# A diffusion backbone step on one core: a weight split that asks for its own load only, and four steps a unit for the last part of the S5 build

## The chip, the cores and the metric

The kernel runs on one core of a Trainium2 chip, in one launch. The metric is the time of one execution on the device in microseconds (us), the median of several runs. In this text PE is the matrix engine (TensorE), PEld its weight loads, DVE the vector engine, ACT the scalar engine, POOL GpSimd, and SP the engine that does nothing here but issue DMAs. Every engine works through its own instructions in the order in which they stand; so does SP: a DMA that must wait for its buffer holds up every DMA behind it.

## The reference, cut to what matters

One step of a two-layer network over 640 tokens (128 context tokens and 512 latent ones) of width 1024. Everything is float32.

```
for layer in (0, 1):
    mod = silu(cond) @ ada_w[layer] + ada_b[layer]        # 6 vectors of 1024 for each of two conditions
    h = rmsnorm(x) * (1 + scale) + shift
    if layer == 0:
        y = [pooling mixer | gated short convolution](h @ ab_w_in) @ ab_w_out
    else:
        q, k, v, u = split(h @ cd_w_in)
        y = [attention(q, k, v) | gelu, glu of S5(u)] @ cd_w_out
    x = x + gate * y
    x = x + gate2 * (relu(h2 @ mlp_w1) ** 2 @ mlp_w2)
```

S5 is a linear recurrence in both directions with complex coefficients: `state[t] = lam_bar * state[t-1] + b_bar @ u[t]`, `y[t] = Re(c @ state[t]) + d * u[t]`. Its matrices are parameters of the layer and depend on no token.

## The kernel before, in words

**Layout.** The activations stand transposed in SBUF, eight chunks of 128 features by 640 tokens, the tokens in two halves of 320. The weights come in 178 units of 128x1024 (512 KB each), used in a fixed order. Each float32 product is made of three fast ones: the unit's high part `wh` and low part `wl`, and the same of the activation, in the order (wl, high), (wh, high), (wh, low). A whole unit is 48 matmuls of 320 columns, a half of one 24.

**The stream of weights.** `load` (L249) issues on SP the DMAs of the next units into tiles `raw` (two buffers; units 2 and 3 have buffers of another tag), as far as `ahead` units beyond the next to be split. `split` (L258) takes the next unit: ACT copies `raw` into `wh` (L266), and `wl = raw - wh` follows on DVE (L271) for the units listed in `ON_VECTOR`, on POOL (L273) for the others. There are four `wh`/`wl` pairs, so a unit is split when the unit four places before it is retired. `turn(u)` (L293) is what the main loops call after unit u: it calls `load()` first, then splits without loading further. Other callers are `retire` from `in_units` (L505) and from `glu`, and the start-up (`start`, L541), which splits units 0 to 3 by hand.

**The order of the work.** Each engine's instructions stand in the order in which the Python code emits them. Layer 0: units 0 to 15 (input projection), 16 to 23 (output projection), 24 to 87 (the MLP in four blocks of 16 units). The last block's second half is units 80 to 87: `out_units` (L459) takes 80 to 83 whole, then 84 to 87 once for the first half of the tokens and once more for the second. After every residual add the square of the new x is summed for the norm: ACT squares (L391), POOL adds (`acc`, L392). Layer 1: units 88 to 91 give the S5 input u (`in_units`), 92 and 93 the first q and k, 94 to 97 the v projection, the rest the other q and k with attention between them.

**The S5 build.** The matrices of the recurrence are built from the parameters while the MLP of layer 0 runs. `s5_build` (L936) is a generator; each `yield` ends a small step. Between two MLP units the loop's `step` pumps it 2 or 3 steps (4 while the coefficients are not built). Its last part, from the `store()` after the loop over b (L1044) on, rearranges 1 MB through DRAM: eight DMAs `ast<-kst` (L1047), then for f = 0 to 7 a load `at<-ast` (L1053), a copy on POOL that permutes it (`a2`, L1058; the profile names it a), and a DMA `ast2<-a2` back to DRAM (L1016). The tiles `at` and `a2` have two buffers each. What is not done when the MLP ends is emitted in one piece by `n.pump(1000)`, before `layer1`.

**The entry of layer 1.** `layer1` (L1065) issues on SP, behind what is left of the build: the cached keys and values, four tiles `et` of the build's result, the load of unit 93, and two stores `xst` that put half of x away. `in_units` then runs units 88 to 91; its evacuation writes u to DRAM in another order (`uds<-uf`, issued by ACT, L1216) and reads it back (`up<-uds`, SP, L1220), a chunk of 128 rows at a time. Unit 92's eight k steps have the first S5 products between them: `s5_in(b)` (L1236) multiplies `et` by `up` on PE (L1242) into one of two PSUM banks, ACT (L1247) and DVE (L1249) empty the bank, and SP loads `et` of b + 4. `s5_in` 0 to 3 stand at k = 5, 6, 7 and 7 of unit 92, 4 to 15 in pairs at k = 1 to 6 of unit 93.

Of the kernel before, what the change touches and what calls it, by code (L numbers as in the profile page):

```python
# [205 lines left out]
class Net:  # L206
# [51 lines left out]
    def split(self, ahead=True):  # L258
        u = self.n_split
        if u == self.n_units or len(self.wt) == 4:  # L260
            return
        self.load()
        raw = self.raw.pop(u)
        wh = self.ws.tile([128, 1024], F32R, name="wh")
        wl = self.ws.tile([128, 1024], F32R, name="wl")
        self.nc.scalar.activation(wh, raw, AF.Copy)  # L266
        self.wt[u] = (wh, wl)
        self.n_split += 1
        if u in ON_VECTOR:
            self.pend.add(u)  # L270
            self.defer(lambda: self.nc.vector.tensor_sub(wl, raw, wh.bitcast(F32)))  # L271
        else:
            self.nc.gpsimd.tensor_sub(wl, raw, wh.bitcast(F32))  # L273
        if ahead:
            self.load()
# [671 lines left out]
    def s5_build(self):  # L947
# [66 lines left out]
        def store():  # L1014
            for o, i in stores:
                nc.sync.dma_start(o, i)  # L1016
            stores.clear()

        F = None
        for b in range(17):  # L1020
# [12 lines left out]
            if b < 16:  # L1033
# [8 lines left out]
                cplx(F, self.pa, self.bc[:, 2:4], 2 * b, 1)  # L1042
                yield
        store()  # L1044
        yield
        for t in range(8):
            nc.sync.dma_start(ast[:, t], self.kst[:, :, 16 * t:16 * t + 128].rearrange("n g c -> g n c"))  # L1047
# [500 lines left out]
def _emit(tc, A):  # L1548
    from contextlib import ExitStack
    with ExitStack() as ctx:  # L1550
        n = Net(tc, A, ctx)
        pts = n.start()
        n.bg = n.s5_build()

        n.step = lambda: n.ada_step(1 if n.n_ada < 40 else 0)
        n.built, n.np = False, 1
        n.layer0(pts)

        def step():
            if n.n_ada < 48:  # L1560
                n.ada_step(2)
            else:
                n.spare = None
                n.ada_step(0 if not n.built else 1)
                n.pump(4 if not n.built else 3 if n.np % 8 == 0 else 2)
                n.np += n.built

        n.step = step
        n.mlp(0, 24, n.norm(0, 3, C_N2), n.norm(1, 0, C_N1))
        n.ada_step(96)  # L1570
        n.pump(1000)
        n.step = lambda: None
        n.layer1(88, n.norm(1, 0, C_N1), n.norm(1, 3, C_N2))
        n.step = lambda: n.late(2)
        n.mlp(1, 114, n.norm(1, 3, C_N2), n.final)
        n.stats_half(1)
        n.spread()
        n.final(1, range(KC))
# [15 lines left out]
```

## Time and profile before

| what | value |
|---|---|
| time, median of 3 runs | 1484.7 us |
| lowest, highest | 1480.81, 1505.91 us |
| the profiled execution's own time | 1483.03 us |
| its span in the trace | 1481.3 us |
| PE busy | 1428.6 us (96% of the span) |
| DVE, POOL, ACT busy | 882.5, 587.8, 484.7 us |
| HBM traffic | 170.5 MB read, 22.5 MB written |

The span is the time from the first to the last instruction of the profiled execution; 1.7 us of its own time lie around it. A busy PE is not PE at full pace: its clock, the granted clock of the profile, has two levels, 1.0 (2.4 GHz) and 0.5 (1.2 GHz), and a stretch's value is a mean of the two. Waits of PE show as idle time, half pace only as a lower clock.

### The profile page before, as it was taken

What the parts mean: (1) busy time and instruction counts of PE and PEld (TensorE: products, weight loads), DVE (VectorE), ACT (ScalarE), POOL (GpSimd) and SP (SyncE); (2) the same over time, 40 slices, a digit from 0 to 9 for tenths busy, and PEclk for the clock granted to TensorE, in tenths of its full rate; (3) what the DMA queues carried; (4) which work ended last, traced back from release to release, by engine and by line L of the source; (5) the groups of instructions that cost most, each with busy time, mean ns of one, the idle gap of its engine ahead of it and who ended that gap; (6) DMA issues with size and microseconds to landing.
All of it is one profiled execution on the core that took longest, in us unless ns stands there. A gap on an engine that the chain in (4) does not pass through costs nothing.

```text
span 1481.3 us, 24120 instructions
## 1 busy us (share of the span) xinstructions
PE 1428.6 (96%) x9757; PEld 1397.0 (94%) x9757; DVE 882.5 (60%) x1618; ACT 484.7 (33%) x856; POOL 587.8 (40%) x429
## 2 busy tenths in 40 slices
PE   7999999999999999999989999999999999999997
PEld 7999899999999999999988888998999999999996
DVE  7899986889988888844539764427541211211213
ACT  4321234312423432433433445535322312311321
POOL 2333021326788679734324321050433333333341
PEclk9999999999999999999999999999999999999998
DMA  9245531514544545524673323521532222222211
GB/s 377 86 174 175 185 129 59 186 57 142 194 173 152 176 169 175 178 83 155 224 219 127 99 80 101 201 72 58 169 116 72 72 86 72 72 81 76 73 58 71
DMA packets 73966, 193.30 MB, mean 131 GB/s; under 512 B 15360, under 2 KB 23936, under 8 KB 73344
## 3 DMA queue, kind: packets, MB, share of 16 engines
q1 hardware_dynamic: 68976, 188.99, 37.8%
q10 hardware_dynamic: 4880, 2.78, 0.6%
q8 instruction: 77, 1.26, 0.4%
q14 instruction: 33, 0.27, 0.1%
HBM read 170.51 MB, written 22.54 MB: 130 GB/s over the span
## 4 chain that ended last, share of the span: by engine, by line
PE 73%; DVE 13%; issue 5%; ACT 3%; POOL 2%; DMA 2%; SPq 0%; ACTq 0%; DVEq 0%; POOLq 0%
PE pp L304 64%; DVE condb L335 3%; PE bk L1437 2%; DVE wl L271 1%; PE pp L1319 1%; DVE x L449 1%; PE pp L1504 1%; PE bk L1242 1%; DVE hl L443 1%; PE pp L1419 1%; ACT wh L266 1%; PE pp L1391 1%; DMA raw<-wts 1%; PE bk L999 1%; DVE pb L681 1%
## 5 line engine op out<-in xcount | busy, mean ns | idle before, releaser
L273 POOL TENSOR_TENSOR wl<-raw,wh 128x1024 fp32r<-128x1024 f32 x112 | 277.3, 2480 | 605.2 <-ACT wh L266 545.0
L304 PE MATMUL pp<-hh,wl 128*128 128x320 f32 x1472 | 360.6, 316 | 9.7 <-ACT hh L437 6.3
L304 PE MATMUL pp<-hl,wh 128*128 128x320 f32 x1472 | 355.4, 312 | 2.2 <-DVE hl L636 2.0
L304 PE MATMUL pp<-hh,wh 128*128 128x320 f32 x1472 | 354.3, 311 | 0.0
L266 ACT ACTIVATE wh<-raw 128x1024 fp32r<-128x1024 f32 x178 | 186.3, 1051 | 327.3 <-PE pp L304 234.0
L304 PE MATMUL pp<-dh,wl 128*128 128x320 f32 x1152 | 280.1, 310 | 5.6 <-DVE x L449 2.7
L304 PE MATMUL pp<-dh,wh 128*128 128x320 f32 x1152 | 278.0, 309 | 0.0
L304 PE MATMUL pp<-dl,wh 128*128 128x320 f32 x1152 | 278.0, 309 | 0.0
L304 PEld LDWEIGHTS pp<-hh,wl 128*128 128x128 f32 x1472 | 251.9, 190 | 14.1 <-ACT hh L437 7.0
L304 PEld LDWEIGHTS pp<-hl,wh 128*128 128x128 f32 x1472 | 252.9, 190 | 3.7 <-DVE hl L636 2.8
L304 PEld LDWEIGHTS pp<-hh,wh 128*128 128x128 f32 x1472 | 253.0, 190 | 0.0
L449 DVE SCALAR_TENSOR_TENSOR x<-pp,mod,x 128x128 f32<-128x128 f32 (+2 forms) x240 | 91.5, 433 | 241.6 <-PE pp L304 241.3
L304 PEld LDWEIGHTS pp<-dh,wl 128*128 128x128 f32 x1152 | 195.9, 188 | 8.8 <-issue 5.6
L304 PEld LDWEIGHTS pp<-dl,wh 128*128 128x128 f32 x1152 | 196.6, 188 | 0.3 <-DVE dl L454 0.3
L304 PEld LDWEIGHTS pp<-dh,wh 128*128 128x128 f32 x1152 | 196.5, 188 | 0.0
L335 DVE SCALAR_TENSOR_TENSOR condb<-ada,condb 128x1024 bf16<-128x1024 f32 x124 | 182.7, 1474 | 2.4
L775 DVE SCALAR_TENSOR_TENSOR pp<-pp,t 128x640 f32<-128x640 f32 x64 | 53.1, 830 | 179.9 <-ACT t L774 179.9
L774 ACT ACTIVATE t<-pp 128x640 f32<-128x640 f32 x64 | 45.1, 704 | 253.4 <-PE pp L304 238.5
L392 POOL TENSOR_TENSOR acc<-acc,sq 128x320 f32<-128x320 f32 (+1 forms) x36 | 40.0, 1112 | 129.6 <-ACT sq L391 121.4
L271 DVE TENSOR_TENSOR wl<-raw,wh 128x1024 fp32r<-128x1024 f32 x66 | 90.0, 1363 | 0.0
L391 ACT ACTIVATE sq<-x 128x320 f32<-128x320 f32 (+1 forms) x51 | 29.1, 570 | 113.4 <-DVE x L449 107.0
L777 DVE TENSOR_TENSOR dl<-pp,dh 128x640 fp32r<-128x640 f32 x64 | 52.6, 822 | 3.9 <-DVE pp L775 0.5
(249 smaller groups left out, 1601.2 us busy)
## 6 DMA issues: line engine op xcount, KB each, us to landing
raw<-wts SPq DMA_DIRECT2D x178, 512.0 KB, 3.5
ada<-ada SPq DMA_DIRECT2D x80, 512.0 KB, 4.4
spare<-ada SPq DMA_DIRECT2D x16, 512.0 KB, 3.5
est<-s5e SPq DMA_DIRECT2D x16, 256.0 KB, 4.6
fst<-s5fc SPq DMA_DIRECT2D x16, 256.0 KB, 4.5
et<-est SPq DMA_DIRECT2D x16, 256.0 KB, 3.7
ft<-fst SPq DMA_DIRECT2D x8, 512.0 KB, 4.1
x<-x SPq DMA_DIRECT2D x8, 320.0 KB, 5.2
```

The costliest lines, as they stand in the source:

```text
L266: self.nc.scalar.activation(wh, raw, AF.Copy)
L271: self.defer(lambda: self.nc.vector.tensor_sub(wl, raw, wh.bitcast(F32)))
L273: self.nc.gpsimd.tensor_sub(wl, raw, wh.bitcast(F32))
L304: self.nc.tensor.matmul(o, a[:, w], b[:, s], start=first and n == 0, stop=last and n == 2)
L335: self.nc.vector.scalar_tensor_tensor(self.junk, a, 1.0, self.condb[:, c], op0=OP.mult, op1=OP.mult, accum_out=self.mod[:, l, j, f, c:c + 1])
L391: self.nc.scalar.activation(q, self.x[f][:, s], AF.Square)
L392: (self.nc.vector if f >= last else self.nc.gpsimd).tensor_add(self.acc[:, s], self.acc[:, s], q)
L449: self.nc.vector.scalar_tensor_tensor(self.x[f][:, s], p[:, s.start - 320 * h:s.stop - 320 * h], self.mod[:, l, j, f, c:c + 1], self.x[f][ ...
L774: self.nc.scalar.activation(t, p, AF.Relu)
L775: self.nc.vector.scalar_tensor_tensor(p, p, 0.0, t, op0=OP.max, op1=OP.mult)
L777: self.defer(lambda: self.nc.vector.tensor_sub(dl, p, dh.bitcast(F32)))
L1437: nc.tensor.matmul(po[:, 64 * h:64 * (h + 1)], pT[:, h, 128 * b:128 * (b + 1)], vv[:, hs], start=b == 0, stop=b == len(vs) - 1)
```

## The change

`split` calls `load(1)` where it called `load()`, which is `load(2)`: before it splits unit u it makes sure that unit u is loaded, and no longer issues the load of u + 1. After `turn` it makes no difference, since `turn` has called `load()` itself. And from the end of the build's loop over b on, a new flag `turning` makes `step` pump four build steps where it pumped two or three.

```
     def split(self, ahead=True):
         u = self.n_split
         if u == self.n_units or len(self.wt) == 4:
             return
-        self.load()
+        self.load(1)
...
         store()
+        self.turning = True
         yield
         for t in range(8):
             nc.sync.dma_start(ast[:, t], self.kst[:, :, 16 * t:16 * t + 128].rearrange("n g c -> g n c"))
...
-        n.built, n.np = False, 1
+        n.built, n.turning, n.np = False, False, 1
...
-                n.pump(4 if not n.built else 3 if n.np % 8 == 0 else 2)
+                n.pump(4 if n.turning or not n.built else 3 if n.np % 8 == 0 else 2)
```

PE, DVE and ACT have the same instructions in the same order before and after; only POOL and SP differ, POOL in one place. On POOL, during units 81 to 83 and the half passes of 84 to 87, there stood before (wl of units 85, 86 and 87, the copies L1058, and the sums `acc`):

```order
L273 TENSOR_TENSOR wl_6740<-raw_6706,wh_6739 128x1024
L392 TENSOR_TENSOR acc_6704<-acc_6704,sq_6805 128x640
L273 TENSOR_TENSOR wl_6811<-raw_6737,wh_6810 128x1024
L1058 COPY a2_6816<-at_6751 128x4x8x16
L392 TENSOR_TENSOR acc_6704<-acc_6704,sq_6870 128x640
L273 TENSOR_TENSOR wl_6876<-raw_6808,wh_6875 128x1024
L1058 COPY a2_6882<-at_6814 128x4x8x16
L392 TENSOR_TENSOR acc_6704<-acc_6704,sq_6911 128x320
L392 TENSOR_TENSOR acc_6704<-acc_6704,sq_6941 128x320
```

The same place on POOL now (the copies' line is L1059):

```order
L273 TENSOR_TENSOR wl_6740<-raw_6706,wh_6739 128x1024
L1059 COPY a2_6755<-at_6751 128x4x8x16
L392 TENSOR_TENSOR acc_6704<-acc_6704,sq_6809 128x640
L273 TENSOR_TENSOR wl_6815<-raw_6737,wh_6814 128x1024
L1059 COPY a2_6821<-at_6753 128x4x8x16
L1059 COPY a2_6826<-at_6818 128x4x8x16
L392 TENSOR_TENSOR acc_6704<-acc_6704,sq_6880 128x640
L273 TENSOR_TENSOR wl_6886<-raw_6812,wh_6885 128x1024
L1059 COPY a2_6892<-at_6823 128x4x8x16
L1059 COPY a2_6897<-at_6889 128x4x8x16
L392 TENSOR_TENSOR acc_6704<-acc_6704,sq_6926 128x320
```

The first copy stood behind wl of unit 86 and stands ahead of it now; wl of unit 87 had one copy ahead of it and has three; five copies, where there were two, stand ahead of the six half sums, and three instead of six behind them.

SP's queue at the entry of layer 1 before, from the load of unit 93 on (`raw_7479` and `raw_7485` are units 94 and 95, `raw_7546` is unit 96):

```order
L255 DMA raw_7264<-wts 128x1024
L1089 DMA xst_7246<-x_72 128x1280 x2
L1220 DMA up_7261<-uds_7247 128x8x80 x2
L255 DMA raw_7479<-wts 128x1024
L255 DMA raw_7485<-wts 128x1024
L1220 DMA up_7261<-uds_7247 128x8x80 x2
L255 DMA raw_7546<-wts 128x1024
L1344 DMA attc_7249<-rpb 64x1x265 x4
L1226 DMA et_7596<-est_3223 128x512
```

And now:

```order
L255 DMA raw_7264<-wts 128x1024
L1090 DMA xst_7246<-x_72 128x1280 x2
L1221 DMA up_7261<-uds_7247 128x8x80 x2
L255 DMA raw_7479<-wts 128x1024
L255 DMA raw_7485<-wts 128x1024
L1221 DMA up_7261<-uds_7247 128x8x80 x2
L1345 DMA attc_7249<-rpb 64x1x265 x4
L1227 DMA et_7594<-est_3223 128x512
L1227 DMA et_7610<-est_3223 128x512
L1227 DMA et_7626<-est_3223 128x512
L1227 DMA et_7636<-est_3223 128x512
L255 DMA raw_7651<-wts 128x1024
```

Unit 96's load has moved from ahead of the four `rpb` and the four `et` loads to behind them. Further ahead in the same queue, between the load of unit 92 and the cached keys, 12 DMAs of the build stood before and 6 stand now. In the start-up, unit 3's load has moved from among the `ada` loads to the place where unit 4's stood, and unit 4's to behind the two DMAs that follow.

## Rows read from the trace of the kernel before

**Rows 1.** Windows: us of PE, PEld, DVE, ACT, POOL (instructions), clock, DMA share, GB/s.

```profile
708.00:776.00 68.00, 60.50 (x397) 59.22 (x396) 25.27 (x68) 25.45 (x50) 20.57 (x14) 0.90 0.73 233
```

**Rows 2.** Timeline of POOL, units 82 to 84 (start, duration, operation, idle before).

```profile
671.85 2.39 POOL L273 TENSOR_TENSOR wl<-raw,wh 128x1024 fp32r<-128x1024 f32 x1
679.49 1.19 POOL L1058 COPY a<-at 128x512 f32<-128x512 f32 x1 [5.26 <-DMA at<-ast]
680.52 1.58 POOL L392 TENSOR_TENSOR acc<-acc,sq 128x640 f32<-128x640 f32 x1
682.06 2.39 POOL L273 TENSOR_TENSOR wl<-raw,wh 128x1024 fp32r<-128x1024 f32 x1
684.40 1.18 POOL L1058 COPY a<-at 128x512 f32<-128x512 f32 x1
```

**Rows 3.** Timeline of DVE: the first residual add after units 85 and 86.

```profile
681.45 0.68 DVE L449 SCALAR_TENSOR_TENSOR x<-pp,mod,x 128x128 f32<-128x128 f32 x2 [2.84 <-PE pp L304]
684.97 0.68 DVE L449 SCALAR_TENSOR_TENSOR x<-pp,mod,x 128x128 f32<-128x128 f32 x2 [2.84 <-PE pp L304]
```

**Rows 4.** Timeline of SP's queue: the first and the third at load.

```profile
675.91 0.33 SPq L1053 DMA_DIRECT2D at<-ast  x1
...
680.72 0.32 SPq L1053 DMA_DIRECT2D at<-ast  x1
```

**Rows 5.** The chain that ended last, around the entry of layer 1 (start, us, what).

```profile
718.40 13.21 PE pp L304 x90
...
733.54 7.10 DMA uds<-uf
...
742.06 7.68 DMA raw<-wts
...
751.85 3.29 PE bk L1242 x16
...
758.42 2.26 PE bk L1242 x16
...
761.60 1.74 PE bk L1242 x16
```

**Rows 6.** Timeline of SP's queue before and at the entry of layer 1.

```profile
708.83 0.38 SPq L1053 DMA_DIRECT2D at<-ast  x1
...
729.66 0.38 SPq L255 DMA_DIRECT2D raw<-wts  x1
730.09 1.43 SPq L1089 DMA_DIRECT2D xst<-x  x2
739.38 1.65 SPq L1220 DMA_DIRECT2D up<-uds  x2
...
742.94 2.08 SPq L1220 DMA_DIRECT2D up<-uds  x2
750.92 0.34 SPq L255 DMA_DIRECT2D raw<-wts  x1
751.32 2.72 SPq L1344 DMA_DIRECT2D attc<-rpb  x4
754.15 0.86 SPq L1226 DMA_DIRECT2D et<-est  x2
```

**Rows 7.** DMA issues of the whole run (KB each, median us from issue to landing).

```profile
et<-est SPq DMA_DIRECT2D x16, 256.0 KB, 3.7
...
xst<-x SPq DMA_DIRECT2D x4, 640.0 KB, 9.0
...
ast<-a SPq DMA_DIRECT2D x8, 256.0 KB, 4.6
```

**Rows 8.** Timeline of PE: the first S5 product.

```profile
743.71 0.53 PE L1242 MATMUL bk<-up,et 128*128 128x80 f32 x3 [0.66 <-DMA up<-uds]
```

**Rows 9.** Timeline of ACT, unit 3's split, and the landing times of all weight loads.

```profile
38.80 1.04 ACT L266 ACTIVATE wh<-raw 128x1024 fp32r<-128x1024 f32 x1
...
DMA to landing us min/median/max: 3.4/3.5/8.4
```

More of the change, by code (lines that the diff above doesn't have):

```diff
@@ L261, in split @@
             return
-        self.load()
+        self.load(1)
         raw = self.raw.pop(u)
@@ L1044, in s5_build @@
         store()
+        self.turning = True
         yield
@@ L1555, in _emit @@
         n.step = lambda: n.ada_step(1 if n.n_ada < 40 else 0)
-        n.built, n.np = False, 1
+        n.built, n.turning, n.np = False, False, 1
         n.layer0(pts)
@@ L1564, in step @@
                 n.ada_step(0 if not n.built else 1)
-                n.pump(4 if not n.built else 3 if n.np % 8 == 0 else 2)
+                n.pump(4 if n.turning or not n.built else 3 if n.np % 8 == 0 else 2)
                 n.np += n.built
```

## Prediction, written before the changed kernel ran

> **What bounds the kernel now.** I read the table first: PE is busy for 96% of the span, so what the change is worth is what it adds to or takes from PE's waits, and from its stretches at half pace. The order of the instructions comes next, since it says where anything differs: PE, DVE and ACT stand as before, and only the queues of POOL and SP do not. So I look at the two stretches in which those queues feed PE. In the first, units 85 to 87, PE goes from one half pass to the next without idling: the residual adds that follow units 85 and 86 begin 3.52 us apart [rows 3], which is 24 matmuls at the full-clock spacing of 13.21 / 90 = 0.147 us [rows 5]. POOL, though, makes these units' low parts only just in time: it finishes unit 87's at 682.06 + 2.39 = 684.45, and unit 86 ends at 684.95 [rows 2, 3]. In the second, 708 to 776 us, the mean clock is 0.90 and PE idles 7.5 us [rows 1]. The chain shows why: a store of u that takes 7.10 us, then a weight load that takes 7.68 us, and PE goes on at 751.85 at half pace, 16 small matmuls in 3.29 us where later ones take 1.74 [rows 5].
>
> **The change part by part.**
>
> *Start-up.* Unit 3's load now goes out where unit 4's went, some 10 us later. ACT splits unit 3 at 38.80, and no weight load of the run took longer than 8.4 us [rows 9]; PE needs unit 3 only when units 0 to 2 are through. Units 4 and 5 wait for nothing but their buffers, which are long free. Lowest price: a gain of 1 us, if the `ada` loads behind it land sooner; highest: 1 us lost, if ACT waits at the split. I take 0: DVE sets the pace there and gets the same work.
>
> *The copies on POOL, units 85 to 87.* The first copy now stands ahead of unit 86's low part. Its load goes out at 675.91, when the eight `ast` DMAs have landed [rows 4]; these stand where they stood, so the copy starts at 679.49 as before [rows 2]. Before, POOL had done unit 86's low part by 674.24 and idled 5.26 us for the copy; now the low part waits behind copy and sum. Their durations: copy to 680.52, sum to 682.06, low part to 684.45 [rows 2]. PE wants it at 681.4, when unit 85's half pass ends [rows 3]: a wait of 3.05 us. Then unit 87's low part: second copy 684.4 to 685.5; third copy, whose tile is free again when the first `ast2` store has landed, 681.1 + 4.6 = 685.7 [rows 4, 7], to 686.9; sum to 688.4; low part to 690.8. Unit 86's 24 matmuls take 3.5 us at full clock, to 688.0, or 3.29 / 1.74 times as long at half, to 691.1. Either way unit 87 cannot begin before 690.8, where it began at 684.95. I take 6.0 us lost. Bounds: 3.05, if the third copy waits for nothing and the low part comes with PE; 8, if its tile is 1.5 us later and the half clock goes on into unit 87. Copies four and five stand ahead of the half sums, and end near 693.3; the sums that the norm needs then end near 696, and PE, 6 us late, asks at 697. That hides them; each further microsecond on POOL would cost one. Nothing downstream gives the 6 us back by itself: DVE, ACT and PE follow each other in one chain up to unit 88.
>
> *The shorter tail at the entry of layer 1* (times below are PE's old ones, as if it had not been delayed). From 708.83 on SP had 12 DMAs of the build to see through, five at loads and seven stores; unit 93's load went out at 729.66 [rows 6]. Now two loads and four stores are left: the load out at 708.8, its copy when the store before it has landed (709.2 + 4.6 = 713.8), the next copy at 715, the last store at 716.3, landed at 720.9, whereupon the last `et` tile is free. Unit 93's load goes out near 721.3, some 8 us earlier, and the two `xst` stores behind it. These take 9.0 us [rows 7]: landed near 732 and not 739. The store of u that the chain names was out at 733.54 and landed at 740.64, right behind `xst` (730.09 + 9.0) [rows 5 to 7]. With `xst` out of its way I give it the 4.6 us of the `ast2` stores: landed at 738.1, 2.5 us earlier. The loads of units 94 and 95 are queued behind it and follow by as much: unit 95's at 739.6. I give it 6.5 us, between the 7.68 of the chain and the common 3.5 [rows 5, 9], but near the upper end, since the other chunks of u still cross it: landed at 746.1. After this load PE went on 2.1 us later (749.74 to 751.85): now at 748.2, where it is ready at 746.6 (the first S5 product without its 0.66 us wait [rows 8], then 8 + 8 small and 12 large matmuls).
>
> *Unit 96's load behind `rpb` and `et`.* Before, `rpb` and the next four `et` stood behind that load, which waited for a buffer until 750.92 [rows 6]. Now they follow the last `up` load at 745.0: `et` out at 747.8, landed at 751.5 (3.7 us [rows 7]). `s5_in(4)` wants it at 748.2 + 1.74 + 12 x 0.147 = 751.7, so this wait is gone. What is late next is unit 96 itself: its load stands behind the `et` whose buffer `s5_in(3)` frees, goes out near 750.3, no earlier than before, and lands at 753.8. ACT has that unit's split ahead of the emptying of `s5_in(4)`'s bank, so PE waits at `s5_in(6)`: ready at 754.3, on at 753.8 + 2.1 = 755.9. It was there at 761.60 [rows 5]: 5.7 us gained. Two waits of about 1.6 us remain. PE was at half pace from 751.85 to about 758.4, which cost 3.3 us; if one of the two waits sets it there, that comes back. I charge half of it, 1.6 us, and take 4.1 us gained. Bounds: 0, if the store of u takes 7.1 us still; 8.9, if PE meets no wait at all (752.7 at `s5_in(6)`).
>
> *Sum.* 0 + 6.0 - 4.1 = 1.9 us more. On the profiled execution, 1483.03 us (a span of 1481.3 and 1.7 around it), that is 1484.9; the median of the runs is 1.7 higher, which gives 1486.6. I take 1486.
>
> *A rule that speaks against the gain.* The rows show a store of u that lands with SP's stores, although ACT issues it [rows 5 to 7]. The Trainium skill (DMA: Bandwidth & Descriptors, section Queues, rings and completion order) says that each DMA engine takes turns between the queues that have work, a packet from one and then from the other. By that rule SP's backlog would at most halve the pace of the store, the 7.1 us would have another reason, and an earlier `xst` would not help: that is the slower rival below. The same section says that a completion counts only after every earlier write of that engine, in any queue; by that one the store is done when `xst` is, as the rows have it. I side with the second.
>
> **The rivals.** *Slower, the gain does not come.* Place: the store of u at 733.54. If it takes its 7.1 us whatever SP has done before, units 94 and 95 load as late as they did, ACT stalls in the same place, and only the loss on POOL is left: 6.0 us, 1489 on the profile's basis, 1490.7 on the median's. It decides from a landing of 7 us on. For it: DMA is busy 0.73 of this stretch in any case [rows 1]. Against it: `xst` and the store end together. *Faster, PE meets no wait in S5.* Full gain 8.9 against 6.0: 2.9 us less, 1480.1 to 1481.8. For it: DMA has 8 us more to work ahead in. Against it: unit 96's load, which nothing brings forward. *The copies do not reach PE.* If the first `at` load landed 3 us sooner, both POOL and PE would be as before and 4 us gained, 1479 to 1481. Against it: what it waits for has not moved.
>
> **How the numbers follow.** My forecast has 0.62, with a range of its own of 1482 to 1490: 3.05 to 8 us lost, 2 to 6 gained. The slower rival 0.19, 1489 to 1493. The two faster ones together 0.16, 1478 to 1482. The rest, 0.03, is something I have not seen. The range of 1478 to 1493 holds most of all of them and leaves a little for the spread of single runs, the lowest of which is 3.9 us under the median. A measurement of this kernel tells about 2% from no change, 29.7 us; no case comes near. So: faster by more 0.01, within 0.97, slower by more 0.02, the last for a chain of waits that keeps the clock low.
>
> **What would show it right or wrong.** Right: PE waits about 3 us for POOL's low part near 681.4 and runs at half pace after it; unit 87's half pass begins near 691; the first copy idles POOL for about 9 us; unit 93's load goes out some 8 us earlier against PE; the store of u lands within 5 us; the long wait for ACT at `s5_in(2)` is under 2 us, and a new one at `s5_in(6)` goes back to unit 96's load. Wrong: no wait for POOL near 681, a store of u of 7 us, or a time outside 1478 to 1493.

## The result, and the profile after

The changed kernel ran in 1503.57 us (median of 4 runs, 1492.35 to 1512.54), the kernel before, beside it, in 1484.17 (4 runs, 1480.81 to 1505.91). The ratio after to before is 1.0131, with a 95% interval of 1.0088 to 1.0173. Forecast were 1486 us and a range of 1478 to 1493. The changed kernel is 1.3% slower by this measurement, less than the 2% that the chances were given for, and the forecast was wrong. Its median is the time of no execution, since it lies between two near 1494 us and two near 1512; the ratios further down leave out executions over 1.5% above the fastest of their kernel.

The profiled execution took 1512.54 us, its span 1510.7. It has 29.4 us more of span than the kernel before, nearly all of it in three places. The first 1.8 us are lost ahead of the S5 build, whose first matmul starts at 372.51 us where it started at 370.72. The second place is POOL and the entry of layer 1, 5.4 us. The third is the end of attention, 22 us: there the clock falls. The page shows the third at once. Its line of the granted clock, 40 slices of the span, stands at nine tenths and more except for two slices with a 6 and the last one, which has an 8 before as well. Changed kernel:

```profile
PE 1454.1 (96%) x9757; PEld 1421.8 (94%) x9757; DVE 879.9 (58%) x1618; ACT 484.3 (32%) x856; POOL 589.6 (39%) x429
PEclk9999999999999999999999996699999999999998
```

PE's share of busy time is 96% as before, with 25.5 us more of it: the time was not lost to waits but to matmuls that took longer. Windows of the changed kernel around that place (columns as in [rows 1]):

```profile
912.00:916.00 4.00, 3.31 (x28) 2.75 (x29) 2.01 (x5) 3.43 (x11) 0.88 (x2) 1.00 0.37 144
916.00:918.00 2.00, 1.36 (x9) 0.85 (x8) 1.97 (x6) 1.23 (x4) 1.12 (x2) 1.00 0.00 0
918.00:920.00 2.00, 1.99 (x10) 1.47 (x11) 0.99 (x3) 1.01 (x4) 0.00 (x0) 0.50 0.00 0
920.00:968.00 48.00, 47.25 (x222) 45.96 (x219) 5.21 (x16) 9.19 (x28) 0.00 (x0) 0.50 0.25 74
968.00:972.00 4.00, 4.00 (x25) 4.00 (x25) 1.70 (x3) 3.92 (x7) 0.00 (x0) 0.85 0.63 172
```

The same stretch of the kernel before:

```profile
900.00:915.00 15.00, 13.64 (x114) 11.58 (x113) 9.83 (x24) 10.26 (x35) 6.38 (x7) 1.00 0.38 133
915.00:970.00 55.00, 51.59 (x383) 49.35 (x383) 21.60 (x37) 27.66 (x51) 6.27 (x3) 1.00 0.50 168
```

From 918 to 968 us PE is busy 98% of the time at 1.2 GHz, and comes back to 2.4 GHz only in the 320-column matmuls, which begin at 965.69. What it works on until then are the last tiles of attention (matmuls of 64 to 256 columns) and the S5 output (80 columns). The kernel before does the same work there at full clock throughout. Just ahead of the fall PE has two short waits, and the kernel before has both, of 0.70 and 0.64 us. Timeline of PE, changed kernel, then the kernel before:

```profile
914.98 0.66 PE L1438 MATMUL bk<-vt,pT 128*128 128x64 f32 x4 [0.69 <-ACT pT L1423]
...
917.18 0.33 PE L1446 MATMUL pp<-const,o 128*128 128x128 f32 x1 [0.64 <-DVE o L454]
```

```profile
907.73 0.66 PE L1437 MATMUL bk<-vt,pT 128*128 128x64 f32 x4 [0.70 <-ACT pT L1422]
...
909.93 0.33 PE L1445 MATMUL pp<-const,o 128*128 128x128 f32 x1 [0.64 <-DVE o L454]
```

So no new wait made the clock fall. This is the question for the experiments. First the rows that answer to those of the prediction. POOL in the changed kernel, against [rows 2]:

```profile
669.73 2.41 POOL L273 TENSOR_TENSOR wl<-raw,wh 128x1024 fp32r<-128x1024 f32 x1
681.21 1.16 POOL L1059 COPY a<-at 128x512 f32<-128x512 f32 x1 [9.07 <-DMA at<-ast]
682.22 1.56 POOL L392 TENSOR_TENSOR acc<-acc,sq 128x640 f32<-128x640 f32 x1
683.74 2.35 POOL L273 TENSOR_TENSOR wl<-raw,wh 128x1024 fp32r<-128x1024 f32 x1
686.03 2.10 POOL L1059 COPY a<-at 128x512 f32<-128x512 f32 x2
687.99 1.55 POOL L392 TENSOR_TENSOR acc<-acc,sq 128x640 f32<-128x640 f32 x1
689.51 2.38 POOL L273 TENSOR_TENSOR wl<-raw,wh 128x1024 fp32r<-128x1024 f32 x1
691.83 1.18 POOL L1059 COPY a<-at 128x512 f32<-128x512 f32 x1
695.29 1.20 POOL L1059 COPY a<-at 128x512 f32<-128x512 f32 x1 [2.28 <-DMA ast<-a]
696.32 2.77 POOL L392 TENSOR_TENSOR acc<-acc,sq 128x320 f32<-128x320 f32 x3
```

The first copy idles POOL for 9.07 us, the low part of unit 86 follows at 683.74 where it stood at 671.85, and that of unit 87 ends at 691.89. PE waits for both and then for the half sums. The groups of PE behind these waits start at 686.13, 691.94 and 699.67; the last of the three waits had been costed at nothing:

```profile
686.13 0.64 PE L304 MATMUL pp<-dh,wl 128*128 128x320 f32 x1 [2.95 <-POOL wl L273]
...
691.94 0.41 PE L304 MATMUL pp<-dh,wl 128*128 128x320 f32 x1 [0.60 <-POOL wl L273]
...
699.67 0.88 PE L398 MATMUL bk<-ones,acc 128*128 128x64 f32 x6 [1.31 <-DVE acc L392]
```

From the first matmul of the build to the last of these rows it is 699.67 - 372.51 = 327.16 us, before 690.93 - 370.72 = 320.21: POOL's new order costs 6.95 us.

At the entry of layer 1 everything stands some 8.7 us later than before when it begins (699.67 against 690.93). SP's queue and ACT in the changed kernel, against [rows 6]:

```profile
729.00 0.38 SPq L255 DMA_DIRECT2D raw<-wts  x1
729.43 1.18 SPq L1090 DMA_DIRECT2D xst<-x  x2
743.27 1.45 SPq L1221 DMA_DIRECT2D up<-uds  x2
746.12 2.71 SPq L255 DMA_DIRECT2D raw<-wts  x2
754.24 1.31 SPq L1221 DMA_DIRECT2D up<-uds  x2
755.59 2.73 SPq L1345 DMA_DIRECT2D attc<-rpb  x4
...
758.43 1.80 SPq L1227 DMA_DIRECT2D et<-est  x4
760.33 0.86 SPq L255 DMA_DIRECT2D raw<-wts  x2
```

```profile
741.03 0.34 ACTq L1217 DMA_DIRECT2D uds<-uf  x1
742.18 0.33 ACTq L1217 DMA_DIRECT2D uds<-uf  x1
...
754.66 1.06 ACT L266 ACTIVATE wh<-raw 128x1024 fp32r<-128x1024 f32 x1 [2.88 <-DMA raw<-wts]
...
766.46 1.06 ACT L266 ACTIVATE wh<-raw 128x1024 fp32r<-128x1024 f32 x1 [4.48 <-DMA raw<-wts]
```

Unit 93's load goes out at 729.00 (before 729.66, though PE is 8.7 us later), and the first store of u lands within 2.2 us (741.03 to 743.27). Before, the first took 7.0 us, from 732.40 to the `up` load at 739.38 [rows 6], and the second 7.10 [rows 5]. But unit 96's load, at 760.33, takes until 766.46, and PE waits for ACT, which empties a PSUM bank of S5 only behind that split. PE's last S5 products start at 779.28, 79.61 us behind the row at 699.67; before it was 772.12 - 690.93 = 81.19. In this pair of executions the entry gives back 1.6 us. Timeline of PE, changed kernel:

```profile
768.54 1.98 PE L1243 MATMUL bk<-up,et 128*128 128x80 f32 x16 [2.27 <-ACT S L1248]
...
779.28 1.91 PE L1243 MATMUL bk<-up,et 128*128 128x80 f32 x16
```

and of the kernel before:

```profile
690.93 0.78 PE L398 MATMUL bk<-ones,acc 128*128 128x64 f32 x6
...
772.12 1.91 PE L1242 MATMUL bk<-up,et 128*128 128x80 f32 x16
```

### The profile page after: what moved, and what is told of

Its sections match the earlier page's. It is cut to its first block, busy times and chain, and to the rows that moved or that the text cites. A ratio compares the mean times of both kernels' runs of the same rounds, so it can differ in the third digit from the quotient of the medians.

```text
span 1510.7 us, 24119 instructions
## 1 busy us (share of the span) xinstructions
PE 1454.1 (96%) x9757; PEld 1421.8 (94%) x9757; DVE 879.9 (58%) x1618; ACT 484.3 (32%) x856; POOL 589.6 (39%) x429
## 4 chain that ended last, share of the span: by engine, by line
PE 66%; DVE 17%; issue 7%; ACT 3%; DMA 3%; POOL 2%; SPq 0%; ACTq 0%; DVEq 0%; POOLq 0%
PE pp L304 58%; DVE condb L335 4%; DVE wl L271 2%; PE pp L1505 2%; PE bk L1438 2%; DMA raw<-wts 1%; DVE x L449 1%; DVE hl L443 1%; PE pp L1420 1%; PE pp L1503 1%; DVE S L1271 1%; DVE up L1269 1%; ACT wh L266 1%; DVE up L1270 1%; PE bk L1243 1%
```

## The experiments

All runs below are compared by three distances in the profile, which leave out what happens in the first 370 us: **S** from the first matmul of the build to the first sum over the norm (before 320.2, changed 327.2), **E** from there to the last S5 product of PE (81.2, 79.6), **A** from there to the last product of the S5 output (164.0; changed 185.6, with the fall). The executions of each kernel form a lower group, and in some kernels an upper one some 20 us above, from 1500 us on; the groups are named with each run. In the experiments every execution of an upper group has a mean granted clock of 0.963 to 0.974, every one of a lower group 0.977 to 0.990. Profiles of two upper ones exist, both of the changed kernel, and both show the fall at the end of attention.

**The changed kernel again, and its two parts.** First the changed kernel unaltered:

> The changed kernel once more, unaltered. Its trace shows PE on half clock from 917 to 968 us, in the last attention tiles and the S5 output, where the kernel before kept full clock; that is about 21 of the 29 us between the two traces, and queues account for only some 5.5. Theory 1 (a fall that some runs have and others not): the single runs fall into two groups, near 1490 with a mean clock of 0.985 and near 1511 with 0.968, and the kernel before shows the same two groups some 5 to 8 us lower, its upper one rarer. Theory 2 (the change brings the fall about): nearly all runs of this kernel lie near 1511 and none of the kernel before above 1490.

Measured in 8 executions: four at 1489.05 to 1494.09, four at 1510.93 to 1516.81; ratio 1.0076 (1.0029 to 1.0122). The profile fell on one of the upper ones and shows 0.53 from 915 to 970 us again. Of the kernel before, 31 executions: 23 at 1479.77 to 1490.57, 8 at 1504.66 to 1510.23. So the kernel before has the upper group too. Its 1505.91 in the table ahead of the prediction lies there. Theory 1 holds.

Then the split's own load alone:

```
         u = self.n_split
-        self.load()
+        self.load(1)
```

> Only load(1) in split; the S5 build is pumped as before. POOL stands as in the kernel before. Theory 1: no wait of PE for POOL's low part near 683; the tail of the build is long again, so units 94 and 95 load late as before and PE waits about 4 us at s5_in(2), while the et loads behind are earlier and unit 96's later; low group within 3 us of the kernel before (1481 to 1487), and an upper group about 20 us above it if runs fall into it. Theory 2: if load(1) brings the fall about, most runs are near 1505; if the four steps do, none is.

Measured: 1484.82 us (12 runs), nine at 1480.93 to 1485.44 and three from 1502.44 on; ratio 1.0003 (0.9972 to 1.0035). S 320.2, no wait for POOL. E was 83.6, with unit 96's load behind `rpb` and `et` as in the changed kernel: in this execution the reordering alone brings nothing.

Then the four steps alone, with `load()` in the split:

```
+        self.turning = True
...
+                n.pump(4 if n.turning or not n.built else 3 if n.np % 8 == 0 else 2)
```

> Only the four steps; split calls load() as before, so unit 96's load stands ahead of rpb and et again. Theory 1: PE waits 3 us for POOL's low part of unit 86 near 683 and loses 6 to 7 us up to unit 88, as in the changed kernel; at s5_in(2) it gains some 4 us; low group 1486 to 1492, an upper group about 20 us above it. Theory 2: if the four steps bring the fall about, most runs lie near 1510; if load(1) does, none.

Measured: 1491.90 us (12 runs), eight at 1486.30 to 1493.44, four from 1507.35 to 1514.93; ratio 1.0039 (1.0007 to 1.0071). S 327.1, E 79.7: the loss on POOL comes from the four steps, and so does the small gain at the entry, as far as one execution tells. A was 163.3: the profiled execution had no fall.

**The copies earlier.** To bring all eight copies ahead of the end of the MLP, three steps at every second unit:

```
-                n.pump(4 if n.turning or not n.built else 3 if n.np % 8 == 0 else 2)
+                n.pump(4 if n.turning or not n.built else 3 if n.np % 2 == 0 else 2)
```

> The changed kernel with three build steps at every second unit instead of every eighth, so that the build ends some units earlier: all eight copies stand ahead of the norm's sums on POOL and nothing of the build is left at the entry of layer 1. Theory 1: no wait for POOL's low part and none for the norm's sums near 698 (7 us back against the changed kernel), unit 93's load goes out as soon as its buffer is free; low group near 1480 to 1485, at or a little under the kernel before; upper group 20 us above it if runs fall into it. Theory 2: as long as load(1) and the four steps are in, most runs stay in the upper group, near 1503.

Measured: 1489.02 us (12 runs), eight at 1484.39 to 1489.32, four at 1510.75 to 1512.13; ratio 1.0027 (1.0012 to 1.0042). No wait for POOL near 683 and E 76.8, but S 332.1. Some of that is only its start, since at this pace the build's first matmul stands 5 us earlier, at 365.4; counted from the first sum over a norm, near 210 us, it is 485.8 to the sum near 697, where the kernel before took 480.8. What the faster pace costs is waits of PE for POOL where the matrices are built, 3.9 us against 1.0, one row of it being

```profile
376.09 0.47 PE L999 MATMUL bk<-s5f,bd 128*64 128x144 f32 x4 [1.87 <-POOL s5f L968]
```

**The waits at the end of attention.** Unread products, meant to fill them, in the changed kernel:

```
+            if i == 16:                                   # trans(i), ahead of out(i - 2)
+                for _ in range(2):
+                    nc.tensor.matmul(pt[:, 1, 384:512], self.ident, self.const[:, :128], start=True, stop=True)
...
+            if i in (15, 18):                             # pv(i), ahead of its products
+                nc.tensor.matmul(po[:, 128:432], self.ident, self.const, start=True, stop=True)
```

> The changed kernel, with PE's short waits at the end of attention filled by products that nobody reads: one of 304 columns ahead of the value products of tiles 15 and 18, two of 128 columns ahead of the transposition that tile 16 begins with. At full clock they last 0.51, 0.51 and 2 x 0.21 us, where PE waited 0.71, 0.58 and 0.64 us. Theory A, these waits set off the fall of the clock from 917 to 968 us: no execution of some 12 lies above 1505 us, and the others stay at 1489 to 1495. Theory B, the fall comes by chance in any execution, whatever PE waits for there: a third to a half of the executions lie at 1510 to 1517 as before. In either case the executions without the fall cost 0 to 1 us more than those of the changed kernel.

And one of them lengthened:

```
+            for _ in range(4 if i == 14 else 1):
                 nc.vector.tensor_mul(o, ...)
```

> The changed kernel, with one of these waits made longer: the scaling of tile 14's output on DVE (0.28 us) is done four times over, so the transposition behind it waits some 1.5 us where it waited 0.64. Theory A: nearly all executions lie at 1510 to 1518, and the profile shows a clock of 0.50 from 917 to 968. Theory B: the share above 1505 stays at a third to a half, and the others are 0.8 us longer, 1490 to 1496.

Measured, with the products: eleven executions at 1487.33 to 1497.36, none from 1500 to 1520 (a twelfth, at 1730.31 us with a mean clock of 0.75, resembles no other run and is left aside); ratio 1.0047 (1.0024 to 1.0070). Lengthened: all twelve at 1488.78 to 1496.56; ratio 1.0050 (1.0029 to 1.0070). The kernel before on the same chip had 10 of 30 above 1504. Theory A fell with the lengthened wait, since that should have made the fall certain; theory B fell with both.

The trace shows that the products fill only the waits at tiles 15 and 18. Those of tile 16 write into the PSUM tile of the transposition behind them, and the wait of 0.64 us is still there, now ahead of them: they are work added behind that wait, some 0.5 us of it. PE with the products:

```profile
912.01 0.71 PE L1418 MATMUL pp<-const 128*128 128x128 f32 x4 [0.64 <-DVE o L454]
```

The windows of the kernel with the lengthened wait show what happens there:

```profile
916.00:918.00 2.00, 1.36 (x12) 1.22 (x11) 1.93 (x4) 0.72 (x3) 1.37 (x2) 1.00 0.01 4
918.00:920.00 2.00, 1.13 (x6) 1.14 (x7) 1.90 (x7) 0.81 (x4) 0.00 (x0) 0.65 0.00 0
920.00:922.00 2.00, 2.00 (x11) 1.43 (x10) 1.05 (x4) 1.34 (x4) 0.00 (x0) 0.50 0.00 0
922.00:924.00 2.00, 2.00 (x19) 1.89 (x18) 1.67 (x4) 0.82 (x4) 0.00 (x0) 0.99 0.01 4
```

```profile
918.87 0.47 PE L1447 MATMUL pp<-const,o 128*128 128x128 f32 x1 [1.51 <-ACT P L1409]
```

The wait is 1.51 us, the clock falls at 918 as in the changed kernel, but 4 us later it is back, ahead of the S5 output, and it stays. So there are two things: that the clock falls, and that it stays down. The 22 us come from the second.

**The same products in the kernel before, elsewhere, and behind one wait.** In the kernel before:

> The kernel before, with the same unread products in PE's short waits at the end of attention. The two runs before this one left no execution of 23 with the fall of the clock, whether the waits were filled or one of them was made longer, where 6 of 12 of the changed kernel had it. Theory C: whether the clock falls hangs on the exact sequence of PE's work and waits in these 10 us, and any change of it that keeps PE busier or shifts it can take the kernel out of it. Then no execution lies above 1500 us, the others at 1480 to 1491 with a median near 1485, where about a third of the unaltered kernel's lie at 1503 to 1511; the profile from the first product of the build to the last sum is as long as before (320.2 + 81 + 163 us). Rival D: the 23 were luck of the chip on that day, and a third lie above 1500 here too.

Measured: all twelve at 1480.80 to 1490.54, median 1486.13, where the unaltered kernel had 10 of 29 at 1504.23 to 1513.70 and a median of 1487.38; ratio 1.0000 (0.9979 to 1.0020). S 320.4, E 83.9, A 163.9. E is 2.7 us longer than in the profile of the kernel before, although nothing is altered up to there.

In the changed kernel, but at tiles 3, 4 and 6 (`i == 4`, `i in (3, 6)`):

> A control: the changed kernel with the same unread products some 70 us earlier, at tiles 3, 4 and 6 of attention where 15, 16 and 18 had them, so that the program is as much altered but the work and the waits from 900 to 917 us stand as they were. Theory C, the sequence of work and waits in those last 10 us decides: a third to a half of the executions lie above 1503 us again, the others at 1489 to 1496. Rival E, any alteration ahead of it shifts the kernel out of the fall: none above 1503.

Measured: nine at 1491.03 to 1496.17, two at 1513.69 and 1518.76 (11 runs); ratio 1.0071 (1.0047 to 1.0095). The upper group is still there.

In the changed kernel, the two products of 128 columns ahead of tile 16's transposition alone:

> The changed kernel with the two products of 128 columns alone (2 x 0.21 us), ahead of the transposition that tile 16 begins with, where PE waited 0.64 us just before the clock fell; the waits of 0.71 us before it and of 0.58 us behind it are left. Theory C: if this last wait before the fall is the place, no execution lies above 1503 us and the others stay at 1489 to 1496. Rival: it takes both waits, and a third to a half lie above 1503.

Measured: all twelve at 1487.00 to 1494.05; ratio 1.0029 (1.0011 to 1.0048). The windows that showed 0.50 in the changed kernel:

```profile
915.00:970.00 55.00, 51.70 (x399) 49.18 (x400) 23.72 (x43) 29.32 (x64) 3.77 (x3) 1.00 0.47 158
```

Here PE has the three waits of the changed kernel as they were, 0.69, 0.64 and 0.58 us, and the two products stand behind the second:

```profile
919.17 0.71 PE L1418 MATMUL pp<-const 128*128 128x128 f32 x4 [0.64 <-DVE o L454]
```

Rival E falls by the control, though its 2 of 11 are few; rival D falls by repetition. Of the kernels with PE's work or waits altered at tiles 14 to 18, none of some 70 executions lies in the upper group; of those with them unaltered, 22 of 71, and of the kernel before in its four sets of runs 38 of 112. So some 0.5 us of work behind the wait of 0.64 us goes with the absence of the long fall, with every wait left as it was; at a share of 22 in 71, twelve executions without it would come about once in 86 times. That the waits as such make the fall is not shown, and this run speaks against it. Theory C, that the sequence of work and waits decides, stands, but it says no more than that.

**Other places for the copies.** Two steps behind each of the eight half passes, with two or three a unit:

```
                 self.square(f, h)
+                if self.turning:
+                    self.pump(2)
```

> Another place for the last part of the build: two or three steps a unit as in the kernel before, and two steps more behind the sum of each of the eight half passes of units 84 to 87, so that every low part and every sum on POOL stands ahead of the copy that it follows. The split asks for its own load only. Theory 1, what the changed kernel loses is POOL's order and what it gains is the shorter tail at the entry of layer 1: no wait of PE for POOL from 681 to 700, no build left at the entry, unit 93's load at PE's old 712 to 720, and a gain of 3 to 9 us against the kernel before (executions without a fall of the clock at 1476 to 1482). Rival, the stores of u set the entry whatever stands in SP's queue ahead: the waits there stay within 2 us of the kernel before, 1483 to 1486.

Measured: 1489.40 us (12 runs), nine at 1484.23 to 1492.88, three at 1501.59 to 1513.11; ratio 1.0028 (0.9993 to 1.0064). The waits for the low parts are gone, S is 321.9, the rest being 1.14 us for a half sum. But E is 84.2, although nothing of the build is left at the entry: the build's DMAs now hold up the weight loads in SP's queue, and PE waits for a unit's low part itself:

```profile
709.83 0.42 PE L304 MATMUL pp<-hh,wl 128*128 128x320 f32 x1 [1.14 <-DVE wl L271]
```

The forecast gain of 3 to 9 us did not come. The low parts of units 86 and 87 on DVE (`ON_VECTOR` from 86 on), with the unread products at the end of attention:

> The changed kernel with the low parts of units 86 and 87 made by DVE, so that POOL's copies hold up none, and with PE's short waits filled. Theory 1: from the first product of the build to the first sum over the norm 321.5 us (before 320.2, changed kernel 327.2), since the half sums on POOL are still 1.3 us late; the entry of layer 1 keeps its 79.6 us (before 81.2); so level with the kernel before, 1481 to 1491, no execution above 1500. Rival: DVE, 3.4 us a low part, is late with the residual adds instead, and PE waits 2 us or more for it near 685.

Measured: 1490.86 us, all twelve at 1485.03 to 1496.17; ratio 1.0029 (1.0010 to 1.0049). E 81.0 and not 79.6; S 323.8 and not 321.5: DVE was in time, but PE waited 3.25 us for the sums, because the fifth copy waits for a store and the half sums stand behind it:

```profile
690.12 1.17 POOL L1059 COPY a<-at 128x512 f32<-128x512 f32 x1 [1.74 <-DMA ast<-a]
691.14 0.86 POOL L392 TENSOR_TENSOR acc<-acc,sq 128x320 f32<-128x320 f32 x1
```

Last, the kernel before with the unread products and two more steps in each half pass over the second half of the tokens, behind the load and the split:

```
                     self.turn(u0 + f)
+                    if u0 == 80:
+                        self.pump(2)
                     nxt(0, ...)
```

> The kernel before with the waits filled, and two more build steps behind each of the four half passes over the second half of the tokens, each behind the load and the split that belong there: on POOL no low part and none of the first four half sums stands behind a copy that it did not stand behind before. Theory 1: 320.2 us to the first sum over the norm, and an entry of layer 1 of 79 to 80 us (before 81.2), so 1 to 2 us faster than the same without this step, 1479 to 1490. Rival: the weight loads of units 90 to 92 are late behind the build's DMAs, as in the run with two steps in every half pass, where the entry took 84.2 us.

Measured: 1484.97 us, all twelve at 1479.76 to 1487.05; the kernel before beside it 1487.38 (29 runs, up to 1513.70); ratio 0.9986 (0.9969 to 1.0004). S 320.2, E 78.3, A 162.6. In this execution the shorter tail is had without the loss on POOL. A gain against the lower group of before is not shown: the interval reaches over 1, and that group's median is 1484.28. Against the same kernel without the added steps (1486.13) it is 1.2 us. What is plain is that the executions of 1500 us and more are gone. POOL in this kernel, where the copies stand behind the sums:

```profile
694.70 0.88 POOL L392 TENSOR_TENSOR acc<-acc,sq 128x320 f32<-128x320 f32 x1 [5.80 <-ACT sq L391]
695.52 1.23 POOL L1060 COPY a<-at 128x512 f32<-128x512 f32 x1
700.10 0.89 POOL L392 TENSOR_TENSOR acc<-acc,sq 128x320 f32<-128x320 f32 x1 [3.35 <-ACT sq L391]
700.92 1.20 POOL L1060 COPY a<-at 128x512 f32<-128x512 f32 x1
```

## Why the prediction was wrong

**The step that failed** is the one that said which cases there are. "The rest, 0.03, is something I have not seen", and "no case comes near" 2%: the fall at the end of attention is 22 us (S5 output's end 185.62 us behind the entry's, before 163.97), four times what the two queue terms came to together, and two of the first four runs of the changed kernel lie up there, the profiled one among them. Only "a chain of waits that keeps the clock low" was named, at 0.02, without a place or a price. What the runs showed is that the clock can fall and stay down at the end of attention, behind waits that the kernel before has as well. The material was at hand: of the three times of before the highest stood 21 us above the median. The range was widened for "the spread of single runs, the lowest of which is 3.9 us under the median", and the upper side of that spread was not asked about. A third of the executions of the kernel before have such a time. That the change made them more frequent is not shown: 6 of 12 with it, 38 of 112 without; the alterations of e4, e3 and e2 gave 4, 4 and 3 of 12. Every sign that was named as right came; of those named as wrong, only the time did.

**What the change itself costs**, without the fall, is the lower groups' difference: 1492.5 us for the changed kernel against 1485.5 (medians of the 4 and the 23 executions that ran together), 7 us. The forecast was 1.9. Of the 5 us between them, 3.5 lie in two terms:

- *Copies on POOL*, 6.0 lost, bounds 3.05 to 8: measured 6.95. The mechanism came as written: 9.07 us of idle POOL, waits of 2.95 and 0.60 us with half pace between them, unit 87 at 691.94 or 690.1 without the 1.8 us of the start. What failed is "That hides them": the half sums came 1.31 us late, since the fifth copy waited 2.28 us for the store of an earlier one. Unit 87 came 0.7 us sooner than forecast and the sums later, so the term was right to 1 us.
- *Shorter tail at the entry*, 4.1 gained, bounds 0 to 8.9: measured 1.6 in this pair. The steps held up to the store of u: unit 93's load at 720.3 by PE's old time (forecast 721.3), landing of u in 2.2 us (4.6), `s5_in(2)` on at 748.0 (748.2). So the store does not take 7 us whatever stands ahead, and the slower rival is out. The chain broke behind it: `et` went out 2 us later than forecast, and unit 96's load took 6.1 us where 3.5 had been given, so `s5_in(6)` went on at 759.8 and not at 755.9. The step was this landing, "lands at 753.8": in the trace's record of the DMA packets those of the four `et` ahead move first, and the load's own start at 763.15, 2.8 us behind its issue. The 6 to 8 us of units 94 and 95 were the nearer row. The gain itself is not settled: with the same instructions up to there, E is 79.5, 77.9, 79.5, 83.4 and 83.9 us in the profiles of e1, e5, e6, e11 and e12, and for the kernel before it is 81.2 and, with e8, 83.9. In e11 and e12 the clock is 0.67 and 0.52 from 766 to 776 us, behind the wait at `s5_in(6)`, where it is 1.00 in the changed kernel.
- *Start-up*, 0: with the build's pace unaltered, its first matmul stands at 369.1 to 373.7 us in the kernels with the split's own load and at 370.3 to 371.4 in those without it; no difference beyond this spread, and the 1.8 us of the pair above lie within it.
- Some 2 us of the 7 stay unexplained. In two kernels with both parts of the change A is 166 us without a long fall, with longer half-pace stretches after the waits near 825 and 897, in four others 163.4 to 164.5; whether the change makes these likelier was not tried. The spread of E, some 6 us, holds the 2 us as well.

**The rivals.** The lower group's 1492.5 us lies in the range of the slower rival, 1489 to 1493, but by luck: its condition, a store of u of 7 us, did not come. Unit 96's load was named as what speaks against "PE meets no wait in S5", and it was what held PE. "The copies do not reach PE" was wrong as thought. Between the two rules for the store of u the 2.2 us decide nothing, since with `xst` landed nothing shares the DMA engines with it. The trace of the kernel before does not bear out "the store is done when `xst` is": the first store landed at 739.33 us, the second `xst` at 740.16; in e2 both stores landed ahead of their `xst`, 737.10 ahead of 737.77 and 739.46 ahead of 739.65. Nor did the store go at half pace at the worst, as it would by mere turns: its first packet started at 736.02, 3.6 us behind its issue (changed kernel 0.85), and then its packets of 2560 bytes ran among those of `xst`, of 5120.

## What to carry to other kernels

Look at every single time before giving a range: one run of three that lies 20 us above the others is a second way in which the kernel goes, and a profile of a quick execution says nothing of it. An in-order queue that makes both operands and bookkeeping takes extra work only behind what the next consumer needs, and a copy that waits for a DMA holds up all that is queued after it; the place was worth 7 us, the shorter tail 2 in the pair that was compared. Before a wait is called filled, the trace has to show that it is gone. And where a stretch of small matmuls behind short waits has a loss of 20 us in a third of the executions, half a microsecond of unread products there is worth a try: here the loss was gone in all 12 executions with them (e12), at a cost too small to tell.

## What was not expected of the hardware

- PE stayed at 1.2 GHz for 50 us although it was busy 98% of that time, with matmuls of 64 to 256 columns; the clock came back in the 320-column ones. With a longer wait (1.51 us) at the same place it was back within 4 us, on the same kind of work. What decides between the two was not found.
- The fall comes and goes between executions of one program, in about a third of them, and the waits do not tell which: in eight profiles they are 0.69 to 0.71 and 0.64 us, two with the long fall and six without (before, e2, e3, e4, e7, e11). With the same waits and 0.5 us of work behind the second (e12) it did not come in 12 executions.
- A store of u by ACT landed in 2.2 us when `xst` had landed ahead of it and in 7.0 and 7.1 when not [rows 5]; before the first packet of the first one started, half of its time had gone by (3.6 us).
